# Up projection: the low part of every fourth weight piece made by a negating copy and an adding transfer

## The chip, the cores and the metric

The kernel runs on one core of a Trainium2 chip. The metric is the device time of one execution in microseconds (us). Of the kernel before, two runs are shown; their median is 1499.38 us.

## What is computed

One block of a hybrid transformer over 256 tokens of width 2048, in float32: three kinds of attention (forgetting, stick-breaking, and over 256 memory tokens), merged by gates, an output projection, and a gated feed-forward layer with a causal convolution of three taps. The change lies in the feed-forward layer's first product:

```python
D_MODEL, SEQ, D_FF, CONV_W = 2048, 256, 5632, 3

x = x + merged @ w_out[l]
h2 = rms_norm(x, g_ffn[l])
u = causal_depthwise_conv(h2 @ w_up[l], conv_w[l], conv_b[l])   # w_up: 2048 x 11264
u_gate, u_val = jnp.split(u, 2, axis=-1)
x = x + (jax.nn.silu(u_gate) * u_val) @ w_down[l]
```

## The kernel before

Every large product is computed in parts. A float32 matrix is split into a high part, which is the matrix rounded to the matmul format float32r, and a low part, which is the difference, rounded to the same format. The activations are split once and kept; the weights are streamed from memory and split as they come.

The weights come in pieces. A piece has 128 partitions and 1024 columns of float32, 512 KB. The helper `piece` (L130 to L141) makes one:

- L135: SP issues the load of the piece into a buffer `raw`. There are four `raw` buffers (`WBUFS`).
- L136: ScalarE copies `raw` to `hi`, which rounds it. There are four `hi` buffers (`SBUFS`).
- L137: VectorE subtracts `hi` from `raw` and writes `lo`. There are four `lo` buffers.

The order in which one engine gets its instructions comes from the framework's scheduler. It follows the order of the program where several instructions are ready, except for the start of the kernel, where `pin` holds instructions in the order in which they were written. Semaphores are added by the framework: a buffer is written again when its last reader has finished.

The up projection (L729 to L745) goes over 11 blocks of four tiles of 128 output columns (`f0`), and for each over the gate half and the value half (`s`): 22 groups. A group has four banks of PSUM, one for each of its tiles, and goes over the 16 tiles of 128 rows of the weights in steps of two: eight pieces, 176 in all. A piece gives 2 x 4 pairs of matmuls. In each pair the weights are the stationary operand and `hT`, the normalized activations with their high parts (256 columns) and low parts (256 columns) side by side, is the moving one:

```python
nc.tensor.matmul(ps[i], lhsT=hi[:, j, c], rhs=hT[:, k + j, :], start=first, stop=False)                # L739, 512 columns
nc.tensor.matmul(ps[i][:, :S], lhsT=lo[:, j, c], rhs=hT[:, k + j, :S], start=False, stop=last)         # L740, 256 columns
```

After each piece `tick()` lets up to two waiting pieces of other work put their instructions into the program. After a group, its four convolutions are put there: `conv` (L705 to L725) takes the two halves of a bank together (L710 on ScalarE, L712 on VectorE), scales by the norm (L713), applies the taps (L716 on ScalarE, L717 and L718 on VectorE) and then the Silu (L720 on ScalarE), or the product with the gate and the split of the result (L724, L169, L170).

GpSimd makes a few masks in the attention part and has no instruction in the up projection.

Of the kernel before, what the change touches and what calls it, by code (L numbers as in the profile page):

```python
# [9 lines left out]
F32 = mybir.dt.float32  # L10
F32R = mybir.dt.float32r
AF = mybir.ActivationFunctionType
ALU = mybir.AluOpType
# [28 lines left out]
def hybrid_block(  # L42
# [25 lines left out]
    nc = tc.nc  # L68
# [12 lines left out]
    def bank(name):  # L81
        return pp.tile([P, 512], F32, tag="bank", name=name)
# [14 lines left out]
    def later(gen):  # L97
        waiting.append(gen)

    def tick():  # L100
        while waiting and len(active) < WINDOW:
            active.append([waiting.popleft(), 0])
        for a in list(active):
            if a[1] > 0:
                a[1] -= 1
                continue
            try:
                a[1] = next(a[0]) or 0
            except StopIteration:
                active.remove(a)  # L110
# [13 lines left out]
    def pin(ins):  # L124

        if pinned[0]:
            tc.keep_in_program_order(ins)


    def piece(src, a, n, name):  # L130
        raw = wp.tile([P, PIECE], F32, tag="raw", name=f"raw_{name}")
        hi = wp.tile([P, PIECE], F32R, tag="hi", bufs=SBUFS, name=f"hi_{name}")
        lo = wp.tile([P, PIECE], F32R, tag="lo", bufs=SBUFS, name=f"lo_{name}")
        m = a * n
        nc.sync.dma_start(raw[:, :m].rearrange("p (a n) -> p a n", a=a), src)  # L135
        pin(nc.scalar.copy(hi[:, :m], raw[:, :m]))  # L136
        pin(nc.vector.tensor_tensor(lo[:, :m], raw[:, :m], hi[:, :m].bitcast(F32), ALU.subtract))  # L137
        return (
            hi[:, :m].rearrange("p (a n) -> p a n", a=a),
            lo[:, :m].rearrange("p (a n) -> p a n", a=a),  # L140
        )  # L141
# [9 lines left out]
    def product(x_of, w, nk, n0, n, name):  # L151

        ps = [bank(f"{name}_{t}") for t in range(NT)]
        wv = w.rearrange("(k p) n -> p k n", p=P)
        for k in range(0, nk, 2):
            a = min(2, nk - k)
            wh, wl = piece(wv[:, k : k + a, n0 : n0 + n], a, n, f"{name}_{k}")
            order = [(j, t) for j in range(a) for t in range(NT)]
            if k + a == nk:
                order.sort(key=lambda jt: jt[1])  # L160
            for j, t in order:
                passes(ps[t][:, :n], x_of(k + j), t, wh[:, j], wl[:, j], k + j == 0, k + j == nk - 1)
            tick()
        return ps
# [212 lines left out]


    wh, wl = piece(kvw[:, :1, :512], 1, 512, "kv0_0")
    transposed(memT, memres, gmem, 0, "mT")  # L380
    keep_busy(2)
    mem_piece(2)
    wh1, wl1 = piece(kvw[:, :1, 512:], 1, 512, "kv0_1")
    kv_part(0, 0, wh[:, 0], wl[:, 0])
    transposed(memT, memres, gmem, 2, "mT")
# [308 lines left out]
    upv = w_up[0].rearrange("(k p) n -> p k n", p=P)  # L694
# [10 lines left out]
    def conv(ps, f, s):  # L705
        if not pads:
            padded()
        ct = s * FT + f
        cr = cp.tile([P, S], F32, tag="cr", bufs=2, name=f"cr_{f}_{s}")
        nc.scalar.copy(cr, ps[:, S:])  # L710
        u = pads[f % 2]
        nc.vector.tensor_tensor(cr, cr, ps[:, :S], ALU.add)  # L712
        nc.vector.tensor_tensor(u[:, 2:], cr, rbc, ALU.mult)  # L713
        y = cp.tile([P, S], F32, tag="y", bufs=6, name=f"y_{f}_{s}")
        tap = lambda j: taps[:, j, ct : ct + 1]
        nc.scalar.activation(y, u[:, 2:], AF.Identity, scale=tap(2), bias=tap(3))  # L716
        nc.vector.scalar_tensor_tensor(y, u[:, 1 : S + 1], tap(1), y, ALU.mult, ALU.add)  # L717
        nc.vector.scalar_tensor_tensor(y, u[:, 0:S], tap(0), y, ALU.mult, ALU.add)  # L718
        if s == 0:
            nc.scalar.activation(y, y, AF.Silu)  # L720
            ys[f] = y
        else:
            g = ys.pop(f)
            nc.vector.tensor_tensor(g, g, y, ALU.mult)  # L724
            split_to(aT[:, f, :], g)  # L725
        return
        yield

    for f0 in range(0, FT, 4):  # L729
        for s in range(2):  # L730
            ps = [bank(f"u{f0 + i}_{s}") for i in range(4)]
            c0 = s * D_FF + f0 * P
            for k in range(0, KT, 2):
                hi, lo = piece(upv[:, k : k + 2, c0 : c0 + 512], 2, 512, f"u{f0}_{s}_{k}")
                for j in range(2):
                    first, last = k + j == 0, k + j == KT - 1
                    for i in range(4):
                        c = slice(i * P, (i + 1) * P)
                        nc.tensor.matmul(ps[i], lhsT=hi[:, j, c], rhs=hT[:, k + j, :], start=first, stop=False)  # L739
                        nc.tensor.matmul(  # L740
                            ps[i][:, :S], lhsT=lo[:, j, c], rhs=hT[:, k + j, :S], start=False, stop=last
                        )
                tick()
            for i in range(4):
                later(conv(ps[i], f0 + i, s))  # L745
# [121 lines left out]
    for nb, plan in enumerate(plans):  # L867
# [3 lines left out]
        ns, s, e = plan.count("s"), 0, plan.count("s")  # L871
# [54 lines left out]
```

## Time and profile before

| what | value |
|---|---|
| median of the runs shown | 1499.38 us (1497.72 and 1501.03) |
| span of the profiled execution | 1494.4 us |
| median of the runs less that span | 5.0 us |
| TensorE matmul busy | 1483.2 us, 99% |
| VectorE busy | 1014.0 us, 68% |
| ScalarE busy | 794.0 us, 53% |
| GpSimd busy | 16.1 us, 1% |
| memory read and written | 280.23 MB and 2.10 MB, 189 GB/s over the span |

The span goes from the first to the last instruction of one profiled execution; the table gives no separate time for that execution, so the median of the runs is set beside it. Times in the rows are in us unless marked ns. PE is TensorE's matmuls, PEld its loads of stationary weights, DVE VectorE, ACT ScalarE, POOL GpSimd, SP the engine that only issues transfers. A name such as `lo_u` stands for all buffers of that name in the up projection; L137 is line 137 of the kernel. Rows of groups give the busy time, the mean of one in ns, and after the second bar the idle time of the engine ahead of them and what ended it. Matmuls overlap each other in TensorE's pipeline, so their mean is longer than their pace.

### The profile page before, as it was taken

Reading aid. Unit: us, or ns where it says so; the run is one execution under the profiler, and the core shown is the slowest. Engines: PE = TensorE matmul, PEld = TensorE weight load, DVE = VectorE, ACT = ScalarE, POOL = GpSimd, SP = SyncE. Lnnn points to the kernel's source line nnn. Section 1 sums busy time; section 2 is a strip of 40 time slices with the busy share of each in tenths; the row PEclk is TensorE's granted clock in tenths of the full one; section 3 lists DMA queues with packets and bytes.
Section 4 is the critical chain, followed back from the end, with each engine's and each line's share of the span. In section 5 each row is a group of like instructions: output and inputs, shape, how many; then the busy total and the mean of one; then the engine's idle time right before and its main releaser. Section 6 shows DMA issues by size and latency. Waiting matters only on the chain.

```text
span 1494.4 us, 19871 instructions
## 1 busy us (share of the span) xinstructions
PE 1483.2 (99%) x7429; PEld 1255.9 (84%) x7429; DVE 1014.0 (68%) x1465; ACT 794.0 (53%) x1108; POOL 16.1 (1%) x46
## 2 busy tenths in 40 slices
PE   8999999999999999999999999999999999999998
PEld 6888888888888888888888888888888888888777
DVE  5767566555655646555557778777778778987885
ACT  6755454358544444444456556556556656553552
POOL 0000000001000000000000000000000000000000
PEclk9999999999999999999999999999999999999999
DMA  8665475365666666655555665655656565556554
GB/s 291 193 211 158 126 220 167 119 211 164 188 194 210 185 210 203 185 190 190 184 182 183 198 191 184 196 190 184 198 187 191 186 196 183 199 188 228 185 202 140
DMA packets 138543, 283.62 MB, mean 190 GB/s; under 512 B 9275, under 2 KB 18127, under 8 KB 138447
## 3 DMA queue, kind: packets, MB, share of 16 engines
q1 hardware_dynamic: 137118, 280.26, 59.0%
q10 hardware_dynamic: 1328, 2.11, 0.4%
q8 instruction: 58, 0.95, 0.2%
q14 instruction: 39, 0.31, 0.1%
HBM read 280.23 MB, written 2.10 MB: 189 GB/s over the span
## 4 chain that ended last, share of the span: by engine, by line
PE 95%; DMA 2%; ACT 1%; DVE 1%; issue 0%; POOL 0%; SPq 0%; DVEq 0%; POOLq 0%; ACTq 0%
PE u L739 21%; PE u L740 11%; PE g L147 5%; PE g L148 5%; PE g L149 5%; PE x L797 4%; PE x L798 4%; PE x L799 4%; PE s L147 2%; PE s L149 2%; PE f L147 2%; PE f L149 2%; PE s L148 2%; PE f L148 2%; PE o L147 2%; PE o L149 2%
## 5 line engine op out<-in xcount | busy, mean ns | idle before, releaser
L739 PE MATMUL u<-hT,hi_u 128*128 128x512 f32 x1408 | 488.5, 392 | 0.0
L740 PE MATMUL u<-hT,lo_u 128*128 128x256 f32 x1408 | 395.1, 281 | 0.0
L739 PEld LDWEIGHTS u<-hT,hi_u 128*128 128x128 f32 x1408 | 263.3, 187 | 57.3
L137 DVE TENSOR_TENSOR lo_u<-raw_u,hi_u 128x1024 fp32r<-128x1024 f32 x176 | 215.4, 1224 | 116.0 <-ACT hi_u L136 115.9
L740 PEld LDWEIGHTS u<-hT,lo_u 128*128 128x128 f32 x1408 | 266.8, 189 | 0.0
L136 ACT CAST hi_u<-raw_u 128x1024 fp32r<-128x1024 f32 x176 | 184.7, 1050 | 138.4 <-PE u L739 106.5
L137 DVE TENSOR_TENSOR lo_g<-raw_g,hi_g 128x1024 fp32r<-128x1024 f32 x96 | 117.7, 1229 | 101.3 <-ACT hi_g L136 98.8
L136 ACT CAST hi_g<-raw_g 128x1024 fp32r<-128x1024 f32 x96 | 100.7, 1051 | 121.8 <-PE g L148 97.4
L147 PE MATMUL g<-hi_g,xT 128*128 128x512 f32 x384 | 151.1, 393 | 0.0
L149 PE MATMUL g<-lo_g,xT 128*128 128x512 f32 x384 | 149.8, 390 | 0.0
L148 PE MATMUL g<-hi_g,xT 128*128 128x512 f32 x384 | 149.7, 390 | 0.0
L792 ACT CAST hi_d<-raw_d 128x1024 fp32r<-128x1024 f32 (+1 forms) x88 | 86.7, 993 | 74.6 <-PE x L798 38.7
L793 DVE TENSOR_TENSOR lo_d<-raw_d,hi_d 128x1024 fp32r<-128x1024 f32 (+1 forms) x88 | 99.8, 1148 | 16.2 <-ACT hi_d L792 16.2
L797 PE MATMUL x<-hi_d,aT 128*128 128x512 f32 x268 | 104.4, 390 | 0.0
L799 PE MATMUL x<-lo_d,aT 128*128 128x512 f32 x268 | 104.4, 390 | 0.0
L798 PE MATMUL x<-hi_d,aT 128*128 128x512 f32 x268 | 104.4, 390 | 0.0
L149 PEld LDWEIGHTS g<-lo_g,xT 128*128 128x128 f32 x384 | 72.1, 188 | 15.2
L148 PEld LDWEIGHTS g<-hi_g,xT 128*128 128x128 f32 x384 | 72.2, 188 | 14.5
L147 PEld LDWEIGHTS g<-hi_g,xT 128*128 128x128 f32 x384 | 72.2, 188 | 14.6
L137 DVE TENSOR_TENSOR lo_s<-raw_s,hi_s 128x1024 fp32r<-128x1024 f32 (+1 forms) x40 | 44.7, 1118 | 37.2 <-ACT hi_s L136 37.2
L137 DVE TENSOR_TENSOR lo_f<-raw_f,hi_f 128x1024 fp32r<-128x1024 f32 (+1 forms) x40 | 44.7, 1120 | 34.5 <-ACT hi_f L136 33.0
L136 ACT CAST hi_f<-raw_f 128x1024 fp32r<-128x1024 f32 (+1 forms) x40 | 38.5, 966 | 52.5 <-PE f L148 47.6
(318 smaller groups left out, 2554.3 us busy)
## 6 DMA issues: line engine op xcount, KB each, us to landing
raw_u<-in_w_up_dram SPq DMA_DIRECT2D x176, 512.0 KB, 4.0
raw_g<-in_w_in_dram SPq DMA_DIRECT2D x96, 512.0 KB, 3.6
raw_d<-in_w_down_dram SPq DMA_DIRECT2D x88, 512.0 KB, 4.7
raw_f<-in_w_in_dram SPq DMA_DIRECT2D x32, 512.0 KB, 3.5
raw_s<-in_w_in_dram SPq DMA_DIRECT2D x32, 512.0 KB, 3.4
raw_o<-in_w_out_dram SPq DMA_DIRECT2D x32, 512.0 KB, 4.7
raw_kv<-in_w_mem_kv_dram SPq DMA_DIRECT2D x15, 512.0 KB, 5.4
raw_b<-in_w_br_fox_dram SPq DMA_DIRECT2D x12, 512.0 KB, 4.0
```

Source lines behind the costliest of these rows:

```text
L136: pin(nc.scalar.copy(hi[:, :m], raw[:, :m]))
L137: pin(nc.vector.tensor_tensor(lo[:, :m], raw[:, :m], hi[:, :m].bitcast(F32), ALU.subtract))
L147: nc.tensor.matmul(o, lhsT=xh, rhs=wh, start=first, stop=False)
L148: nc.tensor.matmul(o, lhsT=xl, rhs=wh, start=False, stop=False)
L149: nc.tensor.matmul(o, lhsT=xh, rhs=wl, start=False, stop=last)
L739: nc.tensor.matmul(ps[i], lhsT=hi[:, j, c], rhs=hT[:, k + j, :], start=first, stop=False)
L740: nc.tensor.matmul(ps[i][:, :S], lhsT=lo[:, j, c], rhs=hT[:, k + j, :S], start=False, stop=last)
L792: nc.scalar.copy(hi[:, :n], src)
L793: nc.vector.tensor_tensor(lo[:, :n], src, hi[:, :n].bitcast(F32), ALU.subtract)
L797: nc.tensor.matmul(o, lhsT=ah, rhs=w[0], start=first, stop=False)
L798: nc.tensor.matmul(o, lhsT=al, rhs=w[0], start=False, stop=False)
L799: nc.tensor.matmul(o, lhsT=ah, rhs=w[1], start=False, stop=last)
```

## The change

For every fourth piece of the up projection, those with `k` of 6 and 14, VectorE's subtraction is left out. In its place ScalarE writes the negated high part into `lo`, and GpSimd issues a transfer that reads the same weights from memory a second time and adds them to what is in `lo`. The other three pieces of four, and all other products, are made as before.

```diff
-    def piece(src, a, n, name):
+    def piece(src, a, n, name, added=False):
         raw = wp.tile([P, PIECE], F32, tag="raw", name=f"raw_{name}")
         hi = wp.tile([P, PIECE], F32R, tag="hi", bufs=SBUFS, name=f"hi_{name}")
         lo = wp.tile([P, PIECE], F32R, tag="lo", bufs=SBUFS, name=f"lo_{name}")
         m = a * n
         nc.sync.dma_start(raw[:, :m].rearrange("p (a n) -> p a n", a=a), src)
         pin(nc.scalar.copy(hi[:, :m], raw[:, :m]))
-        pin(nc.vector.tensor_tensor(lo[:, :m], raw[:, :m], hi[:, :m].bitcast(F32), ALU.subtract))
+        if added:
+            pin(nc.scalar.activation(lo[:, :m], hi[:, :m].bitcast(F32), AF.Copy, scale=-1.0))
+            nc.gpsimd.dma_start(lo[:, :m].rearrange("p (a n) -> p a n", a=a), src, accum_op=ALU.add)
+        else:
+            pin(nc.vector.tensor_tensor(lo[:, :m], raw[:, :m], hi[:, :m].bitcast(F32), ALU.subtract))
...
             for k in range(0, KT, 2):
-                hi, lo = piece(upv[:, k : k + 2, c0 : c0 + 512], 2, 512, f"u{f0}_{s}_{k}")
+                added = (k // 2) % 4 == 3
+                hi, lo = piece(upv[:, k : k + 2, c0 : c0 + 512], 2, 512, f"u{f0}_{s}_{k}", added)
```

## Prediction

> **What bounds the kernel now.** I read the busy times of the page first, then the matmul groups, then the stage of the up projection by itself.
>
> ```profile
> span 1494.4 us, 19871 instructions
> PE 1483.2 (99%) x7429; PEld 1255.9 (84%) x7429; DVE 1014.0 (68%) x1465; ACT 794.0 (53%) x1108; POOL 16.1 (1%) x46
> ...
> L739 PE MATMUL u<-hT,hi_u 128*128 128x512 f32 x1408 | 488.5, 392 | 0.0
> L740 PE MATMUL u<-hT,lo_u 128*128 128x256 f32 x1408 | 395.1, 281 | 0.0
> ...
> L137 DVE TENSOR_TENSOR lo_u<-raw_u,hi_u 128x1024 fp32r<-128x1024 f32 x176 | 215.4, 1224 | 116.0 <-ACT hi_u L136 115.9
> L740 PEld LDWEIGHTS u<-hT,lo_u 128*128 128x128 f32 x1408 | 266.8, 189 | 0.0
> L136 ACT CAST hi_u<-raw_u 128x1024 fp32r<-128x1024 f32 x176 | 184.7, 1050 | 138.4 <-PE u L739 106.5
> ```
>
> ```profile
> core 0: us, PE busy (x) PEld busy (x) DVE busy (x) ACT busy (x) POOL busy (x), PEclk, DMA share, GB/s
> 766.02:1255.50 489.48, 489.48 (x2828) 432.07 (x2827) 366.75 (x607) 289.83 (x444) 0.00 (x0) 1.00 0.60 189
> ```
>
> TensorE is the bound. In the stage of the up projection, 766.02 to 1255.50, it is busy all 489.48 us, at a granted clock of 1.00, and neither of its two lines has a microsecond of idle time in front of it. VectorE is busy 366.75 of those 489.48 us, ScalarE 289.83, GpSimd not at all. The stage eats 176 pieces of weights (x176), so one piece lasts 489.48 / 176 = 2.78 us on TensorE, and four last 11.1 us. Since no matmul is taken away, this stage can't become shorter; VectorE time given back here buys nothing. All that is left to find out is whether the new way of making a low part is late, and by how much.
>
> How much lateness is there room for? The ring of hi and lo buffers has four places, so a high part is copied when TensorE has finished the piece four before it: the largest wait ahead of that copy is "PE u L739" in the row above. The last of the next four fences counts the copies, to give a copy its place in the sequence.
>
> ```profile
> 967.03 1.05 ACT L136 CAST hi_u<-raw_u 128x1024 fp32r<-128x1024 f32 x1 [0.24 <-PE u L739]
> 967.98 1.09 ACT L716 ACTIVATE y<-u,taps 128x256 f32<-128x256 f32 x2
> 968.98 0.62 ACT L710 COPY cr<-u 128x256 f32<-128x256 f32 x2
> 969.80 1.06 ACT L136 CAST hi_u<-raw_u 128x1024 fp32r<-128x1024 f32 x1 [0.20 <-ACT cr L710]
> 970.76 0.72 ACT L720 ACTIVATE y<-y 128x256 f32<-128x256 f32 x2
> 971.96 1.10 ACT L716 ACTIVATE y<-u,taps 128x256 f32<-128x256 f32 x2 [0.48 <-DVE u L713]
> 972.96 1.03 ACT L136 CAST hi_u<-raw_u 128x1024 fp32r<-128x1024 f32 x1
> ...
> 978.12 1.05 ACT L136 CAST hi_u<-raw_u 128x1024 fp32r<-128x1024 f32 x1 [1.72 <-PE u L739]
> ```
>
> ```profile
> 974.53 0.39 PE L739 MATMUL u<-hT,hi_u 128*128 128x512 f32 x1
> 974.76 0.28 PE L740 MATMUL u<-hT,lo_u 128*128 128x256 f32 x1
> ...
> 985.62 0.39 PE L739 MATMUL u<-hT,hi_u 128*128 128x512 f32 x1
> 985.85 0.28 PE L740 MATMUL u<-hT,lo_u 128*128 128x256 f32 x1
> ```
>
> ```profile
> 968.11 1.23 DVE L137 TENSOR_TENSOR lo_u<-raw_u,hi_u 128x1024 fp32r<-128x1024 f32 x1 [0.20 <-ACT hi_u L136]
> ```
>
> ```profile
> 757.00:967.00 210.00, 78.69 (x75) 1.00 0.60 191
> 757.00:978.10 221.10, 82.88 (x79) 1.00 0.60 189
> ```
>
> 75 copies lie before 967.03 and 79 before 978.12. With eight pieces to a group, counted from 0, these are number 75 = 9 x 8 + 3 and number 79 = 9 x 8 + 7: exactly the two kinds of piece that the change touches. TensorE comes to piece 75 at 766.02 + 75 x 2.78 = 974.5 and to piece 79 at 985.7, which picks the matmul rows 974.53 and 985.62. So from the start of the copy to the first matmul that reads the low part there are 974.76 - 967.03 = 7.73 us and 985.85 - 978.12 = 7.73 us. The weights of that matmul are loaded 0.19 us ahead (PEld row, 189 ns), so the low part must be there 7.5 us after the copy begins. Today it takes 1.05 (copy) + 0.03 (hand-over: 968.11 against 967.03 + 1.05) + 1.22 (VectorE) = 2.3 us, and 5.2 us are spare.
>
> **The change, part by part.** 44 of the 176 pieces change, two in each of the 22 groups.
>
> Removed: 44 subtractions on VectorE of 1.224 us, 53.9 us. VectorE is behind TensorE's back all through the stage, so this is worth 0. The raw buffer of such a piece comes free 1.2 us sooner, because only the copy reads it; no wait of TensorE hangs on it, so 0 again.
>
> Added on ScalarE: 44 negating copies of the size of the high part, 1.05 us each by the L136 row, 46 us in a stage in which ScalarE has 489.5 - 289.8 = 200 us free. They cost nothing as load. Queued behind such a copy on ScalarE are the next pieces' high parts and the convolution's L710, L716 and L720. The densest stretch is the one shown, 967 to 974, and the copies in it can afford it: the one that begins at 972.96 is number 77, read from 766.02 + 77 x 2.78 = 980.1 on. Cost as a delay of others: 0; if the cover were gone, 1.05 us in each group, 22 x 1.05 = 23 us.
>
> Added on GpSimd: 44 transfers of 512 KB that add to what is in SBUF. GpSimd ran nothing in this stage (x0), so nobody queues behind them or waits for GpSimd there. SP's queue keeps its 176 loads and is not passed by anything.
>
> Added wait: TensorE waits at L740 for the landing of the transfer, and everything behind it on TensorE with it. The chain from the start of the copy is 1.05 + 1.05 + three hand-overs of 0.03 = 2.2 us, and then T, the time from the issue of the transfer to its landing. So the stall of a number 7 is x7 = 2.2 + T - 7.5 = T - 5.3. For a number 3 the convolutions of the group that just ended become ready at the same moment; they stand earlier in the program than the negating copy, and the row at 967.98 shows two L716 right behind the high part's copy, 1.09 us. I count them ahead of the negating copy: x3 = x7 + 1.09 (lower bound x7, if the negation goes first; with the two L710 behind them, 0.62, x7 + 1.71). Number 7 has ScalarE to itself (1.72 us idle ahead of 978.12). The added pieces sit always in the same of the four buffers, so a stall is not made up later: the copy of the next such piece starts only when this one has been used.
>
> T is the unknown, since no transfer of this trace adds. The nearest rows:
>
> ```profile
> L135 SPq DMA_DIRECT2D raw_u<-in_w_up_dram x176: 367/368/742, 748.4 to 1235.6; - x176
> ...
> DMA to landing us min/median/max: 3.3/4.0/4.6
> ```
>
> ```profile
> L579 POOL TENSOR_SCALAR_AFFINE_SELECT sb<-sb 128x128 f32<-128x128 f32 x24 | 10.9, 486 | 108.1 <-DVE sb L597 61.8 <-PE g L148 33.0 <-ACT sb L605 13.3
> ```
>
> A plain load of the same 512 KB lands 4.0 us after its issue (3.3 to 4.6). Of this, 0.60 of the 16 engines over 2.78 us, that is 1.66 us, is engine time. An adding transfer has two inputs, the weights and what lies in SBUF: I add one more 1.66 us. It shares the engines with SP's load, which takes 1.66 us out of each 2.78: half a load in the way on average, 0.83. GpSimd starts it in software: a GpSimd instruction of 0.49 us in place of SP's 0.37 adds 0.12. T = 4.0 + 1.66 + 0.83 + 0.12 = 6.6 us. Bounds: below, a plain load at its fastest, 3.3; above, reading the weights, reading SBUF and writing back as three full landings one after the other, 12.0. I take 6.6, nearer to the low end, because the parts of one transfer overlap on 16 engines.
>
> The Trainium skill, "DMA: Bandwidth & Descriptors", section "Anatomy of one DMA — SWDGE (gpsimd) path", fits a transfer issued by GpSimd with 2.0 us plus its bytes at 436 GB/s: for 512 KB some 3.2 us, an estimate, below even the fastest of these loads (3.3). With both inputs counted it would give 4.4 us, less than the 5.3 us that the buffers allow, so by that page the whole change would be free.
>
> Sum: x7 = 6.6 - 5.3 = 1.3, x3 = 1.3 + 1.09 = 2.4; 22 x (1.3 + 2.4) = 81 us. 1494.4 + 81 = 1576 us of span; the median of the runs shown lies 5.0 us above this span (1499.38), so 1581 us. In general the time is 1499.4 + 22 x (2 x (T - 5.3) + 1.09) for T over 5.3. Memory traffic grows by 44 x 512 KB; the engines' share goes from 0.60 to 0.60 x (1 + 0.25 x 2) = 0.90 of the old period, tight but not over.
>
> **The rivals.**
>
> A, hidden, not slower. The one mechanism is a transfer that lands within its allowance: at a T under 5.3 us number 7 never waits. For it: a plain load takes 4.0, and the chain is then 6.2 against 7.5. Against: it would need the second input and the shared engines to cost 1.3 us together, where one more pass alone is 1.66. Its time is 1499 us; with a number 3 late by up to 1.09 us, 1499 to 1523. The limit of 2% (about what a measurement of this kernel can tell from no change), 30 us, is reached at T = 5.4, so this rival decides between "same" and "slower". The rule of the page above would lead here.
>
> B, the addition itself is slow: the transfer holds the engines for four plain loads' time in place of two. Then T = 4.0 + 3 x 1.66 + 0.83 + 0.12 = 9.9 us, x7 = 4.6, x3 = 5.7, and the time 1499.4 + 22 x 10.3 = 1727 us. The engines would need 0.60 x (1 + 0.25 x 4) = 1.20 of the old period, a floor of 587 us for the stage, 98 us more, so it is still the chain that decides. For it: no row shows that adding runs at the speed of copying. Against: the rows have nothing that moves 512 KB so slowly.
>
> By the Trainium skill, "TensorE: Matmul & The Clock Gate", section "Part 1: The HAM clock gate (the "warmup" mystery)", a TensorE idle for about 3.4 us falls to half its clock; in B each stall would then cost more again, and no run here shows such a stall.
>
> C, ScalarE instead of the transfer: T is hidden, but the negating copy pushes the dense stretch behind number 3 by 1.05 us and TensorE feels it once a group, 22 x 1.05 = 23 us, 1522 us. For it: ScalarE works nearly without a break from 967 to 974 in the rows shown. Against: number 77, begun at 972.96 and read at 980.1, has both its parts after 2.3 us and 4.8 us in hand.
>
> D, the change does what it says and gains: VectorE's 53.9 us return as time. Against it stand the 489.48 of 489.48 us of TensorE; a gain of 2% would need 30 us of TensorE work to go, and none goes.
>
> **How the numbers follow.** The forecast, a T of 5.4 to 8 or so: 0.50. A: 0.21. B and slower: 0.25. C: 0.03. D: 0.01. Faster by over 2% is D, 0.01; within 2% is A and C, 0.24; slower is the forecast and B, 0.75. The predicted time is that of the forecast, 1581 us, with its own range 1526 (T = 5.4) to 1643 (T = 8: 22 x 6.5 = 143). The range for 8 in 10 must take in A, so it begins at 1496, and reaches far into B: 1720, a T of 9.8 us.
>
> **What would show each step right or wrong.** In the profile of the changed kernel, PE should wait for DMA lo_u at L740, 44 times, some 1.3 us for number 7 and over 2 us for number 3, about 81 us in total; before, L740 had 0.0. The issue row of lo_u on GpSimd should read about 6.6 us to landing, against about 4.0 to 4.6 for raw_u. VectorE's busy time should fall by 54 us and ScalarE's rise by 46, the stage's DMA share rise to 0.75 or more. A landing under 5.3 us and no wait at L740 makes it rival A, and the forecast wrong in T; a landing of 10 us makes it B. Equal waits for numbers 3 and 7 would refute the 1.09 us of the convolution. A span changed while L740 does not wait would refute the whole mechanism.

## The result, and the profile after

The changed kernel takes 1591.82 us (two runs, 1591.71 and 1591.92) against 1499.38: 6.2% slower, a ratio of 1.062 with a 95% interval of 1.06 to 1.064. That is 92.4 us more. The span of the profiled execution grew from 1494.4 to 1590.2 us.

From the page of the changed kernel, the span, the busy times, two transfer queues, the costliest groups and two issue rows (queue, its packets and megabytes and share of the 16 engines; for issues the size and the median time to landing):

```profile
span 1590.2 us, 20042 instructions
PE 1512.8 (95%) x7429; PEld 1267.8 (80%) x7429; DVE 970.3 (61%) x1421; ACT 833.6 (52%) x1152; POOL 69.3 (4%) x90
...
q1 hardware_dynamic: 137118, 280.26, 57.1%
q0 software_dynamic: 11968, 23.07, 9.4%
...
L744 PE MATMUL u<-hT,hi_u 128*128 128x512 f32 x1408 | 507.9, 403 | 0.0
L745 PE MATMUL u<-hT,lo_u 128*128 128x256 f32 x1408 | 404.3, 287 | 63.3 <-DMA lo_u<-in_w_up_dram 61.0
...
L139 POOL DMA_DIRECT2D lo_u<-in_w_up_dram x44 | 53.1, 1206 | 900.6 <-ACT lo_u L138 625.0
...
raw_u<-in_w_up_dram SPq DMA_DIRECT2D x176, 512.0 KB, 4.4
...
lo_u<-in_w_up_dram POOLq DMA_DIRECT2D x44, 512.0 KB, 6.3
```

TensorE now stands idle for 63.3 us ahead of the low part's matmul (L745; it was L740, with 0.0), and 61.0 of these end when an adding transfer lands. VectorE has 44 us less to do and ScalarE 40 more, and neither shows in the time.

The matmuls of the low part by their tile, before and after (columns: shortest, median, longest in ns; start of the first and of the last), and the spread of the landing times after:

```profile
L740 PE MATMUL u<-hT,lo_u x1408: 277/281/285, 766.2 to 1255.2; 128*128 128x256 f32 x176
```

```profile
L745 PE MATMUL u<-hT,lo_u x1408: 274/280/553, 765.4 to 1346.2; 128*128 128x256 f32 x176
...
DMA to landing us min/median/max: 5.7/6.3/8.6
```

From the first to the last of them it is 489.0 us before and 580.8 after: 91.8 us, so the loss lies in the up projection. (The profiled span grew by 95.8. The other 4 us stand behind the up projection, 239.2 us before and 244.0 after; the run without the transfer below, which is as fast as the kernel before, has 243.2 there.) The longest matmul also went from 285 to 553 ns; that is a second cost, and the timeline shows it. A stall, and TensorE behind it, in the changed kernel:

```profile
785.82 0.39 PE L744 MATMUL u<-hT,hi_u 128*128 128x512 f32 x1
788.05 0.35 PE L745 MATMUL u<-hT,lo_u 128*128 128x256 f32 x1 [1.84 <-DMA lo_u<-in_w_up_dram]
788.24 0.40 PE L744 MATMUL u<-hT,hi_u 128*128 128x512 f32 x1
...
789.77 0.63 PE L744 MATMUL u<-hT,hi_u 128*128 128x512 f32 x1
790.19 0.41 PE L745 MATMUL u<-hT,lo_u 128*128 128x256 f32 x1
...
792.93 0.40 PE L744 MATMUL u<-hT,hi_u 128*128 128x512 f32 x1
```

The low part's matmul should have begun 0.23 us after 785.82 and began 2.23 us after it: 2.0 us lost. From 1.4 us after the stall the matmuls are slow (0.63 and 0.41 in place of 0.39 and 0.28), for some 3.4 us. By stages of that stretch, the column after the busy time being the granted clock:

```profile
782.00:786.00 4.00, 4.00 (x25) 1.00 0.71 143
786.00:788.60 2.60, 0.76 (x5) 1.00 1.08 313
789.47:792.88 3.41, 3.41 (x12) 0.50 0.50 186
```

The clock falls to half for 3.41 us. This happens ten times in the up projection, each time at a stall of number 7, and costs 10 x 3.4 / 2 = 17 us. The starts of the matmuls, one against the next, give the split of the 91.8 us: 74 us in 43 long gaps at the changed pieces, 17 to 18 us in slowed matmuls.

Why ten of the 22 stalls, when others as long did nothing? The ten falls lie whole multiples of 3.413 us apart (the second comes 102.40 us, 30 x 3.413, after the one at 789.47). Cut the trace into fixed stretches of that length, and what counts is TensorE's idle time inside one stretch. Here are the stretches ahead of the falls at 789.47 and 891.87, and a stall without a fall, which a boundary divides:

```profile
786.06:789.47 3.41, 1.57 (x9) 1.00 1.07 341
888.46:891.87 3.41, 1.36 (x8) 1.00 0.94 255
915.76:919.18 3.42, 1.83 (x11) 1.00 0.90 227
919.18:922.59 3.41, 2.88 (x17) 1.00 0.85 279
```

The first two have 3.41 - 1.57 = 1.84 and 3.41 - 1.36 = 2.05 us of idle time. The third stall is as long, but leaves 1.59 us on one side and 0.53 on the other. Over the whole up projection the ten stretches ahead of a fall hold 1.82 to 2.31 us of idle time; of all the others one holds 1.82, and the next 1.66. So whether a stall costs clock depends on where it falls in these stretches as well as on its length.

### The profile page after: what moved, and what is told of

The parts are those of the page before. It is cut to its first block, busy times and chain, and to the rows that moved or that the text cites. A ratio compares the mean times of both kernels' runs of the same rounds, so it can differ in the third digit from the quotient of the medians.

```text
span 1590.2 us, 20042 instructions
## 1 busy us (share of the span) xinstructions
PE 1512.8 (95%) x7429; PEld 1267.8 (80%) x7429; DVE 970.3 (61%) x1421; ACT 833.6 (52%) x1152; POOL 69.3 (4%) x90
## 3 DMA queue, kind: packets, MB, share of 16 engines
q1 hardware_dynamic: 137118, 280.26, 57.1%
## 4 chain that ended last, share of the span: by engine, by line
PE 66%; DMA 20%; ACT 8%; issue 3%; DVE 2%; POOL 0%; SPq 0%; DVEq 0%; ACTq 0%; POOLq 0%
DMA lo_u<-in_w_up_dram 17%; PE u L744 6%; PE g L151 5%; PE g L153 5%; PE g L152 5%; PE u L745 4%; PE x L802 3%; PE x L803 3%; PE x L804 3%; ACT lo_u L138 2%; PE s L151 2%; PE s L153 2%; PE f L151 2%; PE f L153 2%; PE f L152 2%
## 5 line engine op out<-in xcount | busy, mean ns | idle before, releaser
L744 PE MATMUL u<-hT,hi_u 128*128 128x512 f32 x1408 | 507.9, 403 | 0.0
L745 PE MATMUL u<-hT,lo_u 128*128 128x256 f32 x1408 | 404.3, 287 | 63.3 <-DMA lo_u<-in_w_up_dram 61.0
L745 PEld LDWEIGHTS u<-hT,lo_u 128*128 128x128 f32 x1408 | 273.0, 194 | 75.7 <-issue 32.7
L744 PEld LDWEIGHTS u<-hT,hi_u 128*128 128x128 f32 x1408 | 271.5, 193 | 62.0
L141 DVE TENSOR_TENSOR lo_u<-raw_u,hi_u 128x1024 fp32r<-128x1024 f32 x132 | 161.2, 1223 | 158.0 <-ACT hi_u L136 158.0
L139 POOL DMA_DIRECT2D lo_u<-in_w_up_dram x44 | 53.1, 1206 | 900.6 <-ACT lo_u L138 625.0
L716 DVE TENSOR_TENSOR cr<-cr,u 128x256 f32<-128x256 f32 x88 | 36.0, 419 | 52.2 <-ACT cr L714 52.1
```

## The experiments

All are edits of the changed kernel. Each is timed against the kernel before on the same chip, whose medians there were 1497.8 to 1497.9 us. The theory: TensorE misses a deadline, since the low part lands too late after the negating copy. The rivals: ScalarE's extra copy; GpSimd's way of issuing; the extra traffic itself.

**Without the transfer.**

```diff
-            nc.gpsimd.dma_start(lo[:, :m]..., src, accum_op=ALU.add)
+            pin(nc.vector.tensor_tensor(lo[:, :m], raw[:, :m], lo[:, :m].bitcast(F32), ALU.add))
```

> The negating copies stay on ScalarE, and VectorE adds the weights to them in SBUF; GpSimd issues nothing. Theory (the low part lands late): no wait at the low part's matmul, no clock loss, 1499 us, between 1495 and 1505. Rival ScalarE (the negating copy and its place in ScalarE's queue delay TensorE): part of the 92 us stays, over 1520 us.

1498.93 us, ratio 1.0003 (0.9993 to 1.0012). The copies on ScalarE and the low part's matmul in this kernel:

```profile
L138 ACT ACTIVATE lo_u<-hi_u 128x1024 fp32r<-128x1024 f32 x44 | 46.7, 1061 | 0.4
L745 PE MATMUL u<-hT,lo_u 128*128 128x256 f32 x1408 | 394.2, 280 | 0.0
```

44 negating copies of 1.06 us are done and TensorE does not wait. The rival ScalarE is out as a cause by itself: the stalls need the transfer. (The copy and its place in the queue still count in the chain ahead of the transfer, as the working further down shows.)

**A transfer that doesn't add.**

```diff
-            nc.gpsimd.dma_start(lo[:, :m]..., src, accum_op=ALU.add)
+            nc.gpsimd.dma_start(lo[:, :m]..., src)
```

> GpSimd's transfer does not add: it writes the weights over the negated copy, so the low part is wrong. Theory: the second input costs 1.7 us of the 16 engines' time in each transfer; without it T falls from 6.1 to about 4.2 us for number 3 and from 8.0 to about 6 us for number 7; with the 1.4 us by which the negating copy of number 3 starts late, half a microsecond of stall is left for each: about 1520 us, between 1499 and 1540. Rival GpSimd's start (issuing a transfer from GpSimd is slow whatever it does): T stays over 5.5 us for both, over 1560 us.

1510.74 us, ratio 1.0085 (1.007 to 1.01). From its page and its groups:

```profile
q0 software_dynamic: 11968, 23.07, 5.6%
...
L745 PE MATMUL u<-hT,lo_u 128*128 128x256 f32 x1408 | 396.1, 281 | 2.0 <-DMA lo_u<-in_w_up_dram 1.5
L139 POOL DMA_DIRECT2D lo_u<-in_w_up_dram x44 | 31.5, 717 | 843.1 <-ACT lo_u L138 604.9 <-ACT y L724 119.6 <-ACT aT L173 118.6
...
lo_u<-in_w_up_dram POOLq DMA_DIRECT2D x44, 512.0 KB, 4.9
```

The same bytes from the same queue at the same moment land after 4.9 us in the median, not 6.3, and the waits all but vanish. Of the 13 us that stay, 2 are in this wait; the rest was not traced. In engine time, 5.6% of a span of 1509.0 us over 44 transfers is 1.9 us each; in the changed kernel it is 9.4% of 1590.2 over 44, 3.4 us, twice SP's loads there (57.1% of 1590.2 us for 280.26 MB: 1.7 us for 512 KB). So adding takes the engines twice as long as SP's loading, and 1.8 times as long as the plain transfer from GpSimd. GpSimd also issues it more slowly: 1206 ns against 717. The rival GpSimd's start is out as a sole cause.

**One transfer for each group.**

```diff
-                added = (k // 2) % 4 == 3
+                added = k // 2 == 7      # the other kernel: k // 2 == 3
```

> One adding transfer for each group, for number 7 alone. Theory (each stall stands for itself): 22 stalls of 2.0 us and most of the clock loss, 44 + 10: about 1553 us. Rival ring (the stalls of 3 and 7 pass the lateness on to each other): well under half of the 92 us, below 1530, or nearly all of it, over 1575.

> One adding transfer for each group, for number 3 alone. Theory: 22 stalls of 1.4 us and little clock loss, 30 + 3: about 1532 us. Rival ring: below 1515 us, or over 1560.

1535.14 us for number 7 alone (1531.67 to 1542.45, ratio 1.0255, 1.0222 to 1.0288) and 1535.34 us for number 3 alone (ratio 1.0254, 1.0237 to 1.0271). Their waits at the low part's matmul and their landing times, number 7 alone first:

```profile
L745 PE MATMUL u<-hT,lo_u 128*128 128x256 f32 x1408 | 398.7, 283 | 24.4 <-DMA lo_u<-in_w_up_dram 24.1
...
DMA to landing us min/median/max: 5.9/6.6/9.3
```

```profile
L745 PE MATMUL u<-hT,lo_u 128*128 128x256 f32 x1408 | 396.0, 281 | 26.6 <-DMA lo_u<-in_w_up_dram 22.1 <-ACT aT L173 4.5
...
DMA to landing us min/median/max: 5.7/6.0/7.0
```

Number 3 did what was expected (1532): 37.5 us, with no clock loss in its stalls of some 1.4 us each (21 of them, none over 1.7; the first transfer of all is in time). Number 7 alone cost 37 us and not 54: its transfer landed sooner than in company (6.6 in the median; with both, about 8), and the clock fell four times, once for twice as long, not ten. Together they give 75 of the 92 us. The stalls do not pass whole, but a number 7 with a stalled number 3 ahead of it is worse off. Its transfer then has more of SP's packets beside it: between its own first packet and its last, they take 1.76 us of the engines in the changed kernel and 1.15 here (medians), and its own packets spread over 5.6 us there and 4.1 here.

**Small loads beside the transfer.**

```diff
-        nc.sync.dma_start(raw[:, :m]..., src)
-        pin(nc.scalar.copy(hi[:, :m], raw[:, :m]))
+        nc.sync.dma_start(raw[:, : m // 4]..., src[:, :, : n // 4])
+        rv = raw[:, : m // 4].unsqueeze(1).to_broadcast([P, 4, m // 4])
+        pin(nc.scalar.copy(hv, rv))      # hv: hi in four parts; VectorE reads rv too
```

> In the up projection SP loads only a quarter of each piece (128 KB) and the copies read it four times, so the weights are wrong; the adding transfers stay as they are. Theory (SP's loads on the same engines stretch the transfer of number 7 by 1 us for each load that lies beside it): T of number 7 falls from 8.0 to about 6 us, T of number 3 from 6.1 to about 5.8; stalls of 0.4 and 1.1 us and hardly a clock loss: about 1535 us. Rival (the transfer's own speed sets T): T of number 7 stays near 8 us, 1580 us or more.

1543.30 us, ratio 1.0299 (1.0282 to 1.0316). A number 7 in the changed kernel and one here, each in its own stretch:

```profile
DMA to landing us min/median/max: 7.4/7.4/7.4
```

```profile
L146 POOL DMA_DIRECT2D lo_u<-in_w_up_dram x1: 1203/1203/1203, 854.4 to 854.4; - x1
...
DMA to landing us min/median/max: 5.8/5.8/5.8
```

Over all 22, the median time from the issue of a number 7 to the matmul that reads it falls from 8.0 to 6.1 us; that of a number 3 stays at 6.1. From a transfer's first packet to its last, SP's packets take 1.76 us of the engines for a number 7 of the changed kernel, 0.36 for a number 3 there, and 0.35 for a number 7 here; the packets of the three spread over 5.6, 3.7 and 3.7 us. So SP's loads beside it stretch the transfer of number 7 by the 1.9 us between the two kinds. Of the 8 us by which 1535 was missed, 3.4 are two falls of the clock, and some 4 lie in number 3: its stalls stayed at 1.4 us, where 1.1 had been expected.

**Made one piece ahead.**

```diff
-                hi, lo = piece(..., f"u{f0}_{s}_{k}", added)
+                for q in ((k + 2, k) if k % 8 == 4 else () if k in made else (k,)):
+                    made[q] = piece(..., f"u{f0}_{s}_{q}", (q // 2) % 4 == 3)
+                hi, lo = made[k]
```

> The changed pieces are made one piece ahead: number 3 is made before number 2, and number 7 before number 6, in the same four buffers; nothing else changes. Theory (only the deadline is missed): the chain gets 2.78 us more, T stays at 6 to 8 us, the waits at the low part's matmul shrink to a few us or none, no clock loss: about 1500 us, between 1497 and 1510. Rival bandwidth (the second input and the second reading load the engines to 0.9, and that slows TensorE by itself): over 1530 us.

1508.48 us, ratio 1.0067 (1.0052 to 1.0082). The low part's matmul by its group, the issue row, and the stage as a whole:

```profile
L751 PE MATMUL u<-hT,lo_u 128*128 128x256 f32 x1408 | 395.3, 281 | 0.2
```

```profile
lo_u<-in_w_up_dram POOLq DMA_DIRECT2D x44, 512.0 KB, 7.7
```

```profile
766.02:1261.30 495.28, 495.07 (x2822) 431.29 (x2821) 315.91 (x562) 330.77 (x486) 51.81 (x44) 1.00 0.86 233
```

This is the sharpest test. The transfers are all there and land later still (7.7 us in the median), the engines are busier than in any stage before (0.86), and TensorE waits 0.2 us. A deadline moved by one piece, 2.78 us, takes away 82 of the 92 us. About 10 us stay. Some 7 of them are in this stage, 496.0 against 489.0 us from its first matmul of the low part to its last, without an idle TensorE. From 942 us on a piece takes 2.83 us where it took 2.77 before:

```profile
880.00:940.00 60.00, 60.00 (x348) 52.93 (x348) 38.87 (x69) 40.19 (x60) 6.02 (x5) 1.00 0.87 228
960.00:1250.00 290.00, 290.00 (x1644) 251.51 (x1643) 186.27 (x333) 192.74 (x285) 30.26 (x26) 1.00 0.86 233
```

60 us for 348 matmuls are 172 ns each, 290 us for 1644 are 176. The clock is full and the engines are equally busy in both, so their load, the rival bandwidth, is not the cause; pieces of 2.83 us also come in the run with small loads, at a share of 0.45. What sets the pace is open. The other 3 us lie behind the stage (246.5 us to the end, 243.2 in the run without the transfer).

**Matmuls of zeros in the stall.**

```diff
                         nc.tensor.matmul(ps[i], lhsT=hi[:, j, c], rhs=hT[:, k + j, :], start=first, stop=False)
+                        if added and (j, i) == (0, 0):
+                            for _ in range(6):
+                                nc.tensor.matmul(ps[i][:, :384], lhsT=idle[:, :P], rhs=idle, start=False, stop=False)
```

> As the changed kernel, with six matmuls of zeros (384 columns, bf16) added into the same bank between the first two matmuls of each changed piece, so that TensorE is not idle for the first microsecond of the stall. Theory (the lower granted clock comes from the idle time): the clock stays at 1.0, the wait for the low part shrinks by what the six matmuls take, and the time falls by up to the 17 us of slowed matmuls: about 1577 us. Rival traffic (the matmuls are slowed by the extra traffic into SBUF, not by the idle time): clock and time stay, 1590 to 1595 us, or rise.

1576.42 us, ratio 1.052 (1.0497 to 1.0542). The clock of this kernel, and its low part's matmul:

```profile
die 0 (median of its cores): 1577.4 us, clock 1.000
```

```profile
L750 PE MATMUL u<-hT,lo_u 128*128 128x256 f32 x1408 | 397.6, 282 | 23.3 <-DMA lo_u<-in_w_up_dram 22.6
```

264 more matmuls make the kernel 15 us faster, with the traffic unchanged, because the clock stays at full speed. The slowed matmuls were the price of idle time, not of traffic. What remains, 78.5 us, is nearly all lateness: 77 us of it are long gaps between matmuls.

**Every second piece.**

```diff
-                added = (k // 2) % 4 == 3
+                added = (k // 2) % 2 == 1
```

> Every second piece of the up projection gets the adding transfer, 88 in place of 44. Theory (chain): an adding transfer holds the engines 3.4 us and a plain load 1.7 us, so two pieces need 3.4 + 2 x 1.7 = 6.8 us of the engines against 5.55 us of TensorE: the stage is bound by the engines at 88 x 6.8 = 598 us or above it by the waits, since a transfer shares the engines with others all the time and lands after 8 us or more; the stage takes 620 to 760 us, the whole 1630 to 1770 us. Rival (stalls only, no bound by the engines): twice the 92 us, 1590 + 92 = 1684 us, with the DMA share of the stage below 0.9.

1585.57 us, ratio 1.0596 (1.0571 to 1.062): twice the transfers for the price of the single, and both expectations missed. The stage and the low part's matmul:

```profile
766.02:1334.30 568.28, 510.47 (x2820) 433.81 (x2819) 271.74 (x518) 372.53 (x529) 104.72 (x87) 0.99 0.96 244
```

```profile
L745 PE MATMUL u<-hT,lo_u 128*128 128x256 f32 x1408 | 401.1, 285 | 57.8 <-DMA lo_u<-in_w_up_dram 49.2 <-ACT hi_u L136 4.3 <-ACT aT L173 2.3
```

The engines are nearly full (0.96), as the theory had it, but packed so tightly they take less than was put in: 0.96 x 568.28 / 88 = 6.2 us for two pieces, not 6.8, so the bound of 598 us was too high. The waits are not doubled either: 57.8 us for 88 transfers. A reading that fits, and that no run isolates: the four buffers form one ring, and a stall for one piece gives the same time to every other low part in the making, so what counts is the lateness over four pieces (1.6 us here by the long gaps between matmuls, 1.7 in the changed kernel), however many of the four are late.

## Why the prediction was right, and where its steps were off

The forecast was a stall at each changed piece, 81 us in all and 1581 us; it came to 92.4 and 1591.8, inside the likeliest case's own range. TensorE waits for the transfer where it was said to, VectorE's relief is worth nothing, ScalarE's copies cost nothing as load (the run without the transfer), rival A's and B's times did not come. That the sum is so close is luck in part, because errors cancel: number 7 was put 22 x 0.7 = 15 us too low, number 3 22 x 1.0 = 22 us too high, and some 15 us of slowed matmuls were not in it at all.

- **The allowance.** The prediction put the budget at 7.5 us, so T could be 5.3. It placed piece 75 at 974.53 by the average pace, but the stage begins with a few other instructions of TensorE and a slower pace. Counting shows it (matmuls of the high part before the given end, kernel before, and the two rows there):

```profile
766.00:975.20 209.20, 208.34 (x600) 1.00 0.59 187
```

```profile
975.22 0.39 PE L739 MATMUL u<-hT,hi_u 128*128 128x512 f32 x1
975.45 0.28 PE L740 MATMUL u<-hT,lo_u 128*128 128x256 f32 x1
```

600 are 75 pieces of eight, so piece 75 begins at 975.22 and its low part is read 8.4 us after the copy, 0.7 more than the 7.73 counted. The allowance for T was 6.0.

- **T.** 6.6 us forecast, 6.3 in the median. The second input was right: 1.66 forecast, 3.4 - 1.7 = 1.7 measured. (Against the plain transfer from the same queue, 1.9, it is 1.5.) Sharing was not 0.83 for each: next to nothing for number 3, about 1.9 us for number 7. GpSimd's start was put at 0.12 over SP's; its instruction takes 1.2 us where SP's took 0.37, so 0.8. These terms don't close for number 3, 4.0 + 1.7 + 0.8 = 6.5 against 6.0 measured; the difference was not traced.

- **The hand-over to GpSimd.** 0.03 us forecast. A number 7 of the changed kernel:

```profile
856.67 1.06 ACT L138 ACTIVATE lo_u<-hi_u 128x1024 fp32r<-128x1024 f32 x1
```

```profile
858.03 1.20 POOL L139 DMA_DIRECT2D lo_u<-in_w_up_dram  x1 [10.11 <-ACT lo_u L138]
```

858.03 - 856.67 - 1.06 = 0.30 us.

- **Number 3.** Its negating copy does stand behind the convolutions:

```profile
896.34 1.05 ACT L136 CAST hi_u<-raw_u 128x1024 fp32r<-128x1024 f32 x1 [0.25 <-PE u L744]
897.29 1.09 ACT L720 ACTIVATE y<-u,taps 128x256 f32<-128x256 f32 x2
898.29 0.62 ACT L714 COPY cr<-u 128x256 f32<-128x256 f32 x2
898.80 1.06 ACT L138 ACTIVATE lo_u<-hi_u 128x1024 fp32r<-128x1024 f32 x1
```

The copy of the high part ends at 896.34 + 1.05 = 897.39, so the negating one starts 898.80 - 897.39 = 1.4 us late, for 1.09 forecast. Yet the forecast that number 3 waits longer than number 7 was wrong: 1.4 against 2.0 us, because number 7's transfer shares the engines. With the measured terms the working closes. By the medians from issue to read, 6.1 and 8.0, number 3 waits 1.05 + 1.4 + 1.06 + 0.30 + 6.1 - 8.4 = 1.5 and number 7 1.05 + 1.06 + 0.30 + 8.0 - 8.4 = 2.0; the medians of the stalls are 1.4 and 2.0. That is 22 x 3.4 = 75 us, where 81 was forecast.

- **The clock.** The sum had nothing for it; it is worth 15 us (the run with the zeros). The prediction left it to rival B, by the Trainium skill, "TensorE: Matmul & The Clock Gate", section "Part 1: The HAM clock gate (the "warmup" mystery)", which gives an idle time of about 3.4 us. By that rule stalls of 2 to 3 us would be harmless; here ten of 22 were not. The length of the slow spell, 3.4 us, agrees. What the trace adds is the amount: within one fixed stretch of 3.41 us, 1.66 us of idle time were too little, 1.82 went either way, and from 1.84 on the clock fell each time.

- **The rule against the change's cost.** The Trainium skill, "DMA: Bandwidth & Descriptors", section "Anatomy of one DMA — SWDGE (gpsimd) path", gave an estimate of 3.2 us for a transfer from GpSimd, 4.4 with both inputs, by which the change would have been free. Here the plain one took 4.9 in the median and the adding one 6.3: the measurement decides. Sharing is not all of the difference: the plain transfer of number 3, with 0.02 us of SP's packets between its own, still took 4.6 in the median. Where the rest comes from is open.

- **The engines' share.** 0.90 of the old period forecast. In the changed kernel the stage shows 0.77 over 580 us, which is 0.77 x 580 / 489.5 = 0.91.

- **Smaller slips.** The removed subtractions were worth 54 us of VectorE's time and the copies 46.7 of ScalarE's (176 less 132 of 1.22 us, and the L138 row), as forecast; the page's busy times move by 44 and 40, because they count instructions that overlap only once. The lower end of the forecast's range, T = 5.4, is 1528 us by the formula given there, not 1526.

## What to carry to other kernels

Where TensorE never waits, moving work off another engine can't gain; all that counts is whether the new path meets the old deadline, and that is read from one buffer's cycle: when the copy starts, when the product is read, and each hand-over between. If the new path is longer, start it one place earlier in the same ring before anything else is tried: here that took away nine tenths of the loss with no more memory. Place a piece by counting its instructions, not by an average pace, and look at what else is on the transfer engines in the very microseconds of the transfer.

## What the runs showed of the hardware

- An adding transfer into SBUF holds the transfer engines twice as long as a load of the same bytes, 3.4 against 1.7 us for 512 KB (1.9 for a plain transfer from GpSimd), and takes GpSimd 1.2 us to issue against 0.7 for one that doesn't add.
- TensorE's clock fell to half, for 3.41 us, when it had been idle for about 1.8 us within one of a row of fixed stretches of 3.41 us. In the changed kernel the ten stretches ahead of a fall hold 1.82 to 2.31 us, one other 1.82 and the rest at most 1.66; with number 7 alone the stretches ahead of a fall hold 2.05 to 3.02, the others at most 1.75. A stall of 2.1 us that a boundary divided did nothing; stalls of 1.4 us (number 3 alone) never did, and six matmuls of zeros in each stall kept the clock up.
- The matmuls of the up projection ran at one of two paces, 2.77 or 2.83 us for a piece, at full clock and without idle time. With the piece made ahead, both came at a transfer engines' share of 0.86 to 0.87, so that load does not choose between them. What does is open.
